# S5 mixer: the exchanged state inputs from a second product instead of transfers between partitions

## The chip, the core and the metric

The kernel runs on one core of a Trainium2 chip. The metric is the device time of one execution in microseconds (us). TensorE (PE) does the matrix products into PSUM, VectorE (DVE) and ScalarE (ACT) the elementwise work, GpSimd (POOL) a few small operations and some transfers, and SyncE (SP) issues most transfers (DMA). Each engine takes its own instructions in the order of its queue.

## The reference, cut to what matters

Two layers run over 1024 positions of 1024 channels in float32. Layer 0 mixes the positions with S5, layer 1 with a short convolution; after each mixer come a SwiGLU network and a gated embedding. Only the S5 mixer is touched. Each of 64 groups of 16 channels drives 64 complex states:

```python
bu_re = jnp.einsum('bcgk,gpk->bcgp', u_c, bb_re)
bu_im = jnp.einsum('bcgk,gpk->bcgp', u_c, bb_im)
acum_re, acum_im, hl_re, hl_im = lax.associative_scan(
    _scan_combine, (a_seq_re, a_seq_im, bu_re, bu_im), axis=1)
...
y = (jnp.einsum('bcgp,gkp->bcgk', hs_re, c_re)
     - jnp.einsum('bcgp,gkp->bcgk', hs_im, c_im))
```

## The kernel before

The positions are cut into 128 blocks of 8, so that the recurrence runs over 128 block states instead of 1024 positions. The 64 groups are worked through in 8 bands of 8 groups (`GB = 8`, `NBT = 8`, the index is `b`). In a band, the 128 partitions of a state tile hold the 64 real parts (`R0`) and the 64 imaginary parts (`R1`).

For each band these functions are called, in the order of the loop that is printed below:

- `gen_in(b)` (L831) scales and transposes the input into `U` (ACT L836, PE L842, ACT L845), forms the input matrix on DVE (two L575 into `raw`), transposes it on PE (L855, 16 instructions) and copies it out of PSUM on ACT in two halves (L857) into `wbt`.
- `states(b)` (L903) multiplies `wbt` and `U` into `pb`, two PSUM banks (L906, 8 products, each of two instructions).
- `scan(b)` (L909) turns the states into a real recurrence. A rotation by the phase tables `E` needs each part's partner: DVE multiplies `pb` with the sine into `tm` (a `tmp` tile, two L579), two transfers on SP's queue (`swapped`, L641) exchange the upper and lower 64 partitions into `tw`, DVE multiplies `pb` with the cosine into `sv` (two L575) and adds `tw` (one L575). Then eight recurrences (L925) write `gv`, and four more DVE operations rotate back, into a `tmp` tile that outputs read and into `gv`.
- `gen_out(b)` (L859) forms the output matrix `W1` (three L575 of 1024 columns) and, by L874 on PE, L876 on ACT and L880 on POOL, the direct term `kp`. `gen_swap` (L882) makes `W2` by two transfers (L886), `gen_toeplitz` (L889) spreads `kp` into `M` by eight (L893), `gen_phase` (L895) spreads the phase table into `E` by four on POOL's queue (L900). `phases` (L810) makes the table for two bands on DVE.
- `outputs(b)` (L933) sums three products for each group, with `M` (L940), `W1` (L941) and `W2` (L942), 48 PE instructions in a band, and `channels(b, zt)` (L947) transposes the result into the next operand.

`up_product(1)` (L466) is other work of the kernel that has the lowest priority and fills PE in this stage: each piece is six matmuls of 512 columns (L122 to L124 into `pstu`, a pool of one PSUM bank), an ACT copy (L478) and a transfer (L479).

The order within each queue is not written out. The framework's scheduler takes it from a simulated timeline: the instruction that is ready and has the highest priority goes first, and priority falls with the place in the program. PSUM has eight banks: three in pool `tr`, one in `tu`, and two tiles of two banks in `mb`. `gv`, `sv`, `M`, `W2`, `wbt` and `tw` have one buffer each; `U`, `W1`, `E` and `tmp` have two.

After the loop `glu` begins with casts of its weights (L87 into `uhigh`) and TensorE-bound products.

Of the kernel before, what the change touches and what calls it, by code (L numbers as in the profile page):

```python
# [9 lines left out]
F32 = mybir.dt.float32  # L10
# [4 lines left out]
ALU = mybir.AluOpType  # L15
PSUM = bass.MemoryType.PSUM
DRAM = bass.MemoryType.DRAM

P = 128
# [4 lines left out]
def trunk(  # L24
# [8 lines left out]
    V, A, G, PE = nc.vector, nc.scalar, nc.gpsimd, nc.tensor  # L33
# [15 lines left out]
    big = ctx.enter_context(tc.tile_pool(name="big", bufs=1))  # L49
    tr = ctx.enter_context(tc.tile_pool(name="tr", bufs=3, space=PSUM))  # L50
    tu = tc.alloc_tile_pool(name="tu", bufs=1, space=PSUM)
    mb = tc.alloc_tile_pool(name="mb", bufs=2, space=PSUM)
    dram = ctx.enter_context(tc.tile_pool(name="dram", bufs=1, space=DRAM))

    ident = const.tile([P, P], F32, name="ident")
# [26 lines left out]
    def psum(pool=None):  # L82
        pool = pool or mm
        return pool.tile([P, 512], F32, name="ps" + pool.name, tag="ps")
# [7 lines left out]
    def raw_tile(i=None, shape=(P, D), dt=F32, name="raw"):  # L92
        if i is None:
            slots.append(slots.pop(0))
        tag = slots[-1] if i is None else f"r{i}"
        return (uhp if tag == "r3" else rawp).tile(list(shape), dt, name=name, tag=tag)
# [451 lines left out]
    R0, R1 = slice(0, NP), slice(NP, P)  # L548
    GB = P // KG
# [11 lines left out]
    gen = tc.alloc_tile_pool(name="s5g", bufs=1, side="right")  # L561
# [12 lines left out]
    def tt(o, a, b, op):  # L574
        V.tensor_tensor(o, a, b, op)  # L575
        return o

    def stt(o, a, s, b, op0, op1):
        V.scalar_tensor_tensor(o, a, s, b, op0, op1)  # L579
        return o  # L580
# [58 lines left out]
    def swapped(dst, src):  # L639
        for a, c in ((R0, R1), (R1, R0)):  # L640
            nc.sync.dma_start(out=dst[a], in_=src[c])  # L641
# [3 lines left out]
    for hf in range(2):  # L645
        pt = psum(tr)
# [5 lines left out]
    for hf in range(2):  # L652
        pt = psum(tr)
# [148 lines left out]
    sv = run.tile([P, GB, P], F32, name="sv")  # L802
# [4 lines left out]
    def tmp_tile():  # L807
        return run.tile([P, GB * P], F32, name="tmp", tag="tmp", bufs=2)
# [20 lines left out]
    Us, Ws, W2s, Es, Bs, wbts, Ps, kps, Ms = {}, {}, {}, {}, {}, {}, {}, {}, {}  # L829

    def gen_in(b):  # L831

        gsl = slice(b * GB, (b + 1) * GB)
        xg = raw_tile(0).rearrange("p (g t k) -> p g t k", g=GB, t=T)
        for t in range(T):
            A.activation(xg[:, :, T - 1 - t, :], h[t][:, b * P:(b + 1) * P].rearrange("p (g k) -> p g k", k=KG),  # L836
                         AF.Copy, scale=rstd[:, t:t + 1])
        U = Us[b] = run.tile([P, GB, P], F32, name="U", tag="U", bufs=2)
        for hf in range(2):
            pt = psum(tr)  # L840
            for c in range(4):
                PE.transpose(pt[:, c * P:(c + 1) * P], xg[:, 4 * hf + c].rearrange("p t k -> p (t k)"), ident)  # L842
            for c in range(4):
                g = 4 * hf + c
                A.activation(U[:, g, :], pt[:, c * P:(c + 1) * P], AF.Copy, scale=gk[:, b * GB + g:b * GB + g + 1])  # L845
        shp = [P, GB, T, KG]
        Wp = [raw_tile(i).rearrange("p (g t k) -> p g t k", g=GB, t=T) for i in (1, 2)]
        for o, pw, bb in ((Wp[0], pwr, bbA), (Wp[1], pwn, bbS)):
            tt(o, pw[:, gsl, 0:T].unsqueeze(3).broadcast_to(shp), bb[:, gsl].unsqueeze(2).broadcast_to(shp), ALU.mult)
        wbt = wbts[b] = gen.tile([P, GB, P], F32, name="wbt", tag="wbt")  # L850
        for hf in range(2):
            pt = psum(tr)
            for c in range(4):
                for i in range(2):
                    PE.matmul(pt[:, c * P:(c + 1) * P], Wp[i][:, 4 * hf + c].rearrange("p s k -> p (s k)"), ident,  # L855
                              start=i == 0, stop=i == 1, is_transpose=True)
            A.copy(wbt[:, 4 * hf:4 * hf + 4].rearrange("p c n -> p (c n)"), pt)  # L857

    def gen_out(b):  # L859

        gsl = slice(b * GB, (b + 1) * GB)
        shp = [P, GB, NL, KG]
        W1 = Ws[b] = run.tile(shp, F32, name="W1", tag="W1", bufs=2)
        A.copy(W1[:, :, 0, :], cA[:, gsl])
        shp1 = [P, GB, T, KG]
        tm = tmp_tile()[:, 0:GB * P].rearrange("p (g s k) -> p g s k", g=GB, s=T)
        for o, pw, cc in ((W1[:, :, 1:NL, :], pwr, cA), (tm, pwn, cS)):
            tt(o, pw[:, gsl, 1:NL].unsqueeze(3).broadcast_to(shp1), cc[:, gsl].unsqueeze(2).broadcast_to(shp1), ALU.mult)
        tt(W1[:, :, 1:NL, :], W1[:, :, 1:NL, :], tm, ALU.subtract)
        kp = kps[b] = gen.tile([KG, GB, T, KG], F32, name="kp", tag="kp")  # L870
        for hf in range(2):
            pk = psum(tr)
            for c in range(4):
                PE.matmul(pk[0:KG, c * P:(c + 1) * P], bbA[:, b * GB + 4 * hf + c, :], W1[:, 4 * hf + c, 0:T, :],  # L874
                          start=True, stop=True)
            A.copy(kp[:, 4 * hf:4 * hf + 4].rearrange("p g s k -> p (g s k)"), pk[0:KG, :])  # L876
        dd = gen.tile([KG, GB, KG], F32, name="dd", tag="dd")
        G.tensor_tensor(dd, ident[:KG, :KG].unsqueeze(1).broadcast_to([KG, GB, KG]),
                        dk[:, gsl].unsqueeze(2).broadcast_to([KG, GB, KG]), ALU.mult)
        G.tensor_tensor(kp[:, :, 0, :], kp[:, :, 0, :], dd, ALU.add)  # L880
# [20 lines left out]
                                    in_=ptabs[b // LB][two * NP:(two + 1) * NP, :, o:o + HQ, :])  # L901

    def states(b):  # L903
        pb = mb.tile([P, GB * P], F32, name="pb", tag="pb")
        for g in range(GB):
            PE.matmul(pb[:, g * P:(g + 1) * P], wbts[b][:, g, :], Us[b][:, g, :], start=True, stop=True)  # L906
        Bs[b] = pb.rearrange("p (g j) -> p g j", g=GB)

    def scan(b):  # L909
        B = Bs[b]  # L910
        C, S_ = Es[b][:, 0], Es[b][:, 1]
        parts = ((slice(0, NJ - 1), slice(1, NJ), slice(NJ - 1, 0, -1), sgnN, sgnA),
                 (slice(NJ - 1, P - 1), slice(NJ, P), slice(0, NJ), sgnA, sgnN))
        tm = tmp_tile()[:, 0:GB * (P - 1)]
        tv = tm.rearrange("p (g j) -> p g j", g=GB)
        for j, _, m, _, sg in parts:
            stt(tv[:, :, j], B[:, :, j], sg, S_[:, :, m], ALU.mult, ALU.mult)
        tw = gen.tile([P, GB * (P - 1)], F32, name="tw", tag="tw")
        swapped(tw, tm)
        for j, w, m, _, _ in parts:  # L920
            tt(sv[:, :, w], B[:, :, j], C[:, :, m], ALU.mult)
        tt(sv[:, :, 1:P], sv[:, :, 1:P], tw.rearrange("p (g j) -> p g j", g=GB), ALU.add)
        for g in range(GB):
            dec = r8[:, b * GB + g:b * GB + g + 1].broadcast_to([P, P - 1])
            V.tensor_tensor_scan(gv[:, g, 1:P], dec, sv[:, g, 1:P], 0.0, ALU.mult, ALU.add)  # L925
        pv = Ps[b] = tmp_tile().rearrange("p (g j) -> p g j", g=GB)
        G.memset(pv[:, :, 0:1], 0.0)
        for _, w, m, sg, _ in parts:
            tt(pv[:, :, w], gv[:, :, w], C[:, :, m], ALU.mult)
        for _, w, m, sg, _ in parts:  # L930
            stt(gv[:, :, w], gv[:, :, w], sg, S_[:, :, m], ALU.mult, ALU.mult)
# [15 lines left out]
    def channels(b, zt):  # L947
        for hf in range(2):
# [3 lines left out]
            split_pe(v[:, :, b, 0, hf, :], v[:, :, b, 1, hf, :], pt, by_kt)  # L952

    gen_in(0)
    phases(0)
    states(0)
    gen_phase(0)
    gen_out(0)
    gen_swap(0)
    gen_toeplitz(0, M)  # L960
    gen_in(1)
    for b in range(NBT):
        scan(b)
        nx = b + 1
        if nx < NBT - 1:
            if b % LB == 0 and b // LB + 1 < NBT // LB:
                phases(b // LB + 1)
            gen_out(nx)
            zt = outputs(b)
            gen_phase(nx)  # L970
            states(nx)
            gen_swap(nx)
            gen_toeplitz(nx, M)
            if b + 2 < NBT:
                gen_in(b + 2)
            channels(b, zt)
        elif nx < NBT:
            states(nx)
            gen_phase(nx)
            gen_out(nx)  # L980
            M = run.tile([P, GB, P], F32, name="M", tag="E", bufs=2)
            G.memset(M, 0.0)
            gen_toeplitz(nx, M)
            zt = outputs(b)
            channels(b, zt)
            gen_swap(nx)
        else:
            zt = outputs(b)
# [111 lines left out]
```

## Time and profile before

| | us |
|---|---|
| median of 3 runs | 2356.54 |
| lowest and highest | 2355.79, 2357.86 |
| the profiled execution | 2359.43 |
| its span, first to last instruction | 2357.5 |

| engine | busy us | share of the span |
|---|---|---|
| TensorE matmul (PE) | 2247.0 | 95% |
| TensorE weight load (PEld) | 1835.7 | 78% |
| VectorE (DVE) | 1331.9 | 56% |
| ScalarE (ACT) | 765.5 | 32% |
| GpSimd (POOL) | 163.1 | 7% |

Busy times are those of the engines' own instructions. A matmul of 128 columns is shown with 0.27 us or more although the next one starts about 0.11 us after it, so a busy TensorE is not one at its peak. Idle time of an engine that sets no pace costs nothing. The bands of S5 lie between about 55 and 225 us of the span. The profiled execution took 1.93 us more than its span.

### The profile page before, as it was taken

How to read it: one execution, taken by the hardware profiler on the slowest of the kernel's cores; microseconds unless marked ns; L12 is line 12 of the kernel's file. 1: busy time of each engine (PE TensorE's matmuls, PEld its weight loads, DVE VectorE, ACT ScalarE, POOL GpSimd, SP SyncE). 2: the span in 40 equal slices, each digit the busy share in tenths (PEclk: the TensorE clock that was granted, in tenths of full speed). 3: DMA queues.
4: the chain of work that ended last, by engine and by line, in shares of the span. 5: the costliest groups of instructions: out<-in, count | busy, mean ns of one | idle time of the engine just before them, and what ended most of it. 6: DMA issues, size and time to landing. Idle time of an engine off the chain costs nothing.

```text
span 2357.5 us, 27090 instructions
## 1 busy us (share of the span) xinstructions
PE 2247.0 (95%) x10253; PEld 1835.7 (78%) x10253; DVE 1331.9 (56%) x2246; ACT 765.5 (32%) x1449; POOL 163.1 (7%) x268
## 2 busy tenths in 40 slices
PE   6888999899999999999979999989999999999998
PEld 4776887788888878878858888768888888788787
DVE  7785326866666642125488776487666666121454
ACT  6554223433333320013343332153333333000232
POOL 2110001000000000000000000010000001000000
PEclk8999999999999999999989999999999999999999
DMA  7555202333333364333232225434333335543333
GB/s 246 141 135 148 69 1 89 105 112 112 111 114 110 107 241 149 118 127 114 70 129 81 90 92 179 159 125 125 108 108 107 111 113 172 212 139 107 108 109 110
DMA packets 212978, 288.87 MB, mean 123 GB/s; under 512 B 21360, under 2 KB 152432, under 8 KB 212848
## 3 DMA queue, kind: packets, MB, share of 16 engines
q1 hardware_dynamic: 191520, 212.63, 29.0%
q0 software_dynamic: 20928, 74.47, 10.2%
q8 instruction: 80, 1.31, 0.2%
q14 instruction: 50, 0.41, 0.1%
q10 hardware_dynamic: 400, 0.04, 0.0%
HBM read 190.93 MB, written 79.69 MB: 115 GB/s over the span
## 4 chain that ended last, share of the span: by engine, by line
PE 85%; DMA 6%; DVE 5%; ACT 1%; SPq 1%; issue 1%; POOL 0%; DVEq 0%; POOLq 0%; ACTq 0%
PE psmm L122 27%; PE psmm L124 27%; PE psmm L123 27%; DMA ch<-hid 2%; PE pstr L181 1%; DMA raw<-in_ffn_w_out_dram 1%; DMA tw<-tmp 1%; DVE W L575 1%; DVE gv L925 1%; DMA h<-hd 1%; DVE tmp L575 1%; DVE ulow L88 1%; DVE uhigh L88 1%; PE pstr L874 0%; DVE raw L575 0%
## 5 line engine op out<-in xcount | busy, mean ns | idle before, releaser
L122 PE MATMUL psmm<-ulow,ws 128*128 128x512 f32 x896 | 351.1, 393 | 1.6 <-ACT s L301 1.6
L123 PE MATMUL psmm<-ulow,ws 128*128 128x512 f32 x896 | 350.6, 391 | 0.0
L124 PE MATMUL psmm<-ulow,ws 128*128 128x512 f32 x896 | 350.4, 391 | 0.0
L124 PE MATMUL psmm<-uhigh,ws 128*128 128x512 f32 x672 | 265.3, 395 | 0.0
L122 PE MATMUL psmm<-uhigh,ws 128*128 128x512 f32 x672 | 265.1, 394 | 0.0
L123 PE MATMUL psmm<-uhigh,ws 128*128 128x512 f32 x672 | 264.9, 394 | 0.0
L360 DVE TENSOR_TENSOR h<-psmm,h 128x512 f32<-128x512 f32 x128 | 88.0, 690 | 276.6 <-PE psmm L124 276.6
L88 DVE TENSOR_TENSOR ws<-raw,ws 128x512 fp32r<-128x512 f32 x224 | 153.6, 688 | 117.8 <-ACT ws L87 117.4
L87 ACT CAST ws<-raw 128x512 fp32r<-128x512 f32 x224 | 137.5, 619 | 213.0 <-PE psmm L124 211.2
L122 PEld LDWEIGHTS psmm<-ulow,ws 128*128 128x128 f32 x896 | 169.4, 189 | 39.5 <-ACT s L301 2.9
L123 PEld LDWEIGHTS psmm<-ulow,ws 128*128 128x128 f32 x896 | 169.4, 189 | 36.2
L124 PEld LDWEIGHTS psmm<-ulow,ws 128*128 128x128 f32 x896 | 169.2, 189 | 36.2
L87 ACT CAST ws<-st 128x512 fp32r<-128x512 f32 x168 | 104.0, 620 | 204.4 <-PE psmm L124 189.5
L123 PEld LDWEIGHTS psmm<-uhigh,ws 128*128 128x128 f32 x672 | 126.1, 188 | 30.3
L124 PEld LDWEIGHTS psmm<-uhigh,ws 128*128 128x128 f32 x672 | 126.1, 188 | 30.3
L122 PEld LDWEIGHTS psmm<-uhigh,ws 128*128 128x128 f32 x672 | 126.1, 188 | 29.1
L323 POOL DMA_DIRECT2D hid<-hs x104 | 78.2, 755 | 903.4 <-DVE hs L88 895.4
L122 PE MATMUL psmm<-ulow,ch 128*128 128x512 f32 x320 | 128.4, 401 | 10.8 <-DMA ch<-hid 10.8
L139 ACT ACTIVATE junk<-h 128x512 bf16<-128x512 f32 (+1 forms) x113 | 64.0, 567 | 204.0 <-DVE h L360 104.0
L87 ACT CAST uhigh<-raw 128x1024 fp32r<-128x1024 f32 x36 | 37.2, 1049 | 278.9 <-PE psmm L124 136.7
L123 PE MATMUL psmm<-ulow,ch 128*128 128x512 f32 x320 | 127.6, 399 | 0.0
L124 PE MATMUL psmm<-ulow,ch 128*128 128x512 f32 x320 | 127.5, 398 | 0.0
(240 smaller groups left out, 4238.5 us busy)
## 6 DMA issues: line engine op xcount, KB each, us to landing
hid<-hs POOLq DMA_DIRECT2D x104, 512.0 KB, 4.3
ch<-hid SPq DMA_DIRECT2D x96, 512.0 KB, 3.7
raw<-in_ffn_w_in_dram SPq DMA_DIRECT2D x88, 512.0 KB, 4.4
raw<-in_ffn_w_out_dram SPq DMA_DIRECT2D x44, 512.0 KB, 3.6
hd<-h POOLq DMA_DIRECT2D x24, 512.0 KB, 3.0
h<-hd SPq DMA_DIRECT2D x24, 512.0 KB, 8.7
raw<-in_conv_w_in_dram SPq DMA_DIRECT2D x24, 512.0 KB, 4.0
up<-ev SPq DMA_DIRECT2D x32, 256.0 KB, 3.2
```

Source lines behind the costliest of these rows:

```text
L87: A.copy(hi, src)
L88: V.tensor_tensor(lo, src, hi.bitcast(F32), ALU.subtract)
L122: PE.matmul(ps, ahi, bhi, start=start, stop=False, skip_group_check=more)
L123: PE.matmul(ps, ahi, blo, start=False, stop=False, skip_group_check=more)
L124: PE.matmul(ps, alo, bhi, start=False, stop=stop, skip_group_check=more)
L139: A.activation(junk[:, cs], h[t][:, cs], AF.Square, scale=1.0 / math.sqrt(D), accum_out=ms)
L181: PE.transpose(pt[:, c * P:(c + 1) * P], xn[:, kt * P:(kt + 1) * P], ident)
L323: nc.gpsimd.dma_start(out=hid[ht // 4][half * HT:(half + 1) * HT, :, ht % 4].rearrange("t p l j -> p t l j"), in_=hs.bitcast(F32))
L360: V.tensor_tensor(h[t][:, cs], ps[nb], h[t][:, cs], ALU.add)
L575: V.tensor_tensor(o, a, b, op)
L925: V.tensor_tensor_scan(gv[:, g, 1:P], dec, sv[:, g, 1:P], 0.0, ALU.mult, ALU.add)
```

## The change

The input matrix is kept twice: `wbt` as before, and `wbs` with the real and imaginary columns exchanged, which four more ACT copies of 128 x 256 in a band read from the same PSUM tiles. `wbs` takes the buffer of `tw`. `states` makes two products with the same `U`, first `qb` with `wbs`, then `pb` with `wbt`. `qb` and `pb` have one buffer each instead of two of `pb`, so that `mb` keeps four banks. `scan` multiplies `qb` with the sine, with the signs of the other set of `parts`, and adds the result without a transfer.

```diff
-    mb = tc.alloc_tile_pool(name="mb", bufs=2, space=PSUM)
+    mb = tc.alloc_tile_pool(name="mb", bufs=1, space=PSUM)
...
-        wbt = wbts[b] = gen.tile([P, GB, P], F32, name="wbt", tag="wbt")
+        wbt, wbs = wbts[b] = [gen.tile([P, GB, P], F32, name=n, tag=g) for n, g in (("wbt", "wbt"), ("wbs", "tw"))]
...
             A.copy(wbt[:, 4 * hf:4 * hf + 4].rearrange("p c n -> p (c n)"), pt)
+            pv = pt.rearrange("p (c n) -> p c n", c=4)
+            for o, i in ((R0, R1), (R1, R0)):
+                A.copy(wbs[:, 4 * hf:4 * hf + 4, o], pv[:, :, i])
...
     def states(b):
-        pb = mb.tile([P, GB * P], F32, name="pb", tag="pb")
-        for g in range(GB):
-            PE.matmul(pb[:, g * P:(g + 1) * P], wbts[b][:, g, :], Us[b][:, g, :], start=True, stop=True)
-        Bs[b] = pb.rearrange("p (g j) -> p g j", g=GB)
+
+        Bs[b] = []
+        for i, n in ((1, "qb"), (0, "pb")):
+            pb = mb.tile([P, GB * P], F32, name=n, tag=n)
+            for g in range(GB):
+                PE.matmul(pb[:, g * P:(g + 1) * P], wbts[b][i][:, g, :], Us[b][:, g, :], start=True, stop=True)
+            Bs[b].insert(0, pb.rearrange("p (g j) -> p g j", g=GB))
 
     def scan(b):
-        B = Bs[b]
+        B, Bw = Bs[b]
...
-        for j, _, m, _, sg in parts:
-            stt(tv[:, :, j], B[:, :, j], sg, S_[:, :, m], ALU.mult, ALU.mult)
-        tw = gen.tile([P, GB * (P - 1)], F32, name="tw", tag="tw")
-        swapped(tw, tm)
+        for j, _, m, sg, _ in parts:
+            stt(tv[:, :, j], Bw[:, :, j], sg, S_[:, :, m], ALU.mult, ALU.mult)
         for j, w, m, _, _ in parts:
             tt(sv[:, :, w], B[:, :, j], C[:, :, m], ALU.mult)
-        tt(sv[:, :, 1:P], sv[:, :, 1:P], tw.rearrange("p (g j) -> p g j", g=GB), ALU.add)
+        tt(sv[:, :, 1:P], sv[:, :, 1:P], tv, ALU.add)
```

## Rows read from the trace of the kernel before

**Rows 1.** The page: busy time by engine, and the chain that ended last.
```profile
PE 2247.0 (95%) x10253; PEld 1835.7 (78%) x10253; DVE 1331.9 (56%) x2246; ACT 765.5 (32%) x1449; POOL 163.1 (7%) x268
...
PE 85%; DMA 6%; DVE 5%; ACT 1%; SPq 1%; issue 1%; POOL 0%; DVEq 0%; POOLq 0%; ACTq 0%
```

**Rows 2.** Waits of DVE, 55 to 212.8 us: total us, times, longest us.
```profile
DVE sv L575 <- DMA tw<-tmp: 27.1, 8, 5.5
DVE tmp L579 <- DMA E<-ptab: 3.0, 2, 2.1
DVE ptab L813 <- DMA E<-ptab: 2.5, 1, 2.5
DVE raw L575 <- PE pstr L855: 0.3, 1, 0.3
```

**Rows 3.** Timeline of DVE, band 4: start, us, instruction, idle before and releaser.
```profile
138.74 0.74 DVE L579 SCALAR_TENSOR_TENSOR tmp<-pb,sgnA,E 128x504 f32<-128x504 f32 x1
139.51 0.75 DVE L579 SCALAR_TENSOR_TENSOR tmp<-pb,sgnN,E 128x512 f32<-128x512 f32 x1
140.18 1.27 DVE L575 TENSOR_TENSOR sv<-pb,E 128x504 f32<-128x504 f32 x2
146.83 1.22 DVE L575 TENSOR_TENSOR sv<-sv,tw 128x1016 f32<-128x1016 f32 x1 [5.38 <-DMA tw<-tmp]
```

**Rows 4.** Windows: length, busy us (instructions) by engine, granted clock, DMA share, GB/s.
```profile
55.50:212.80 157.30, 132.94 (x949) 113.69 (x947) 124.07 (x246) 82.53 (x207) 23.83 (x49) 0.99 0.60 143
...
126.20:146.80 20.60, 17.17 (x127) 14.96 (x126) 15.18 (x24) 10.83 (x29) 5.70 (x11) 1.00 0.65 160
146.80:167.50 20.70, 18.26 (x136) 15.96 (x135) 19.38 (x46) 11.85 (x33) 1.09 (x3) 1.00 0.43 100
```

**Rows 5.** Timeline of PE: one product of `states`, and what follows it.
```profile
49.90 1.95 PE L906 MATMUL pb<-U,wbt 128*128 128x128 f32 x16
51.60 0.47 PE L122 MATMUL pstu<-ulow 128*128 128x512 f32 x1
```

**Rows 6.** Waits of PE, 55.5 to 212.9 us.
```profile
PE pstr L874 <- DVE W L575: 10.2, 6, 2.4
PE pstr L940 <- DMA W<-W: 5.3, 1, 5.3
PE pstu L122 <- ACT ev L478: 5.1, 5, 1.1
PE pb L906 <- ACT wbt L857: 1.7, 1, 1.7
```

**Rows 7.** Timeline of PE: L874 of band 1 and of band 2, first half.
```profile
72.30 3.50 PE L874 MATMUL pstr<-W,bbA 128*16 128x128 f32 x16 [2.09 <-DVE W L575]
...
94.92 1.03 PE L874 MATMUL pstr<-W,bbA 128*16 128x128 f32 x8
```

**Rows 8.** Groups of ACT, 45 to 225 us, and 225 to 330 us.
```profile
L857 ACT COPY wbt<-pstr 128x512 f32<-128x512 f32 x16 | 9.0, 642 | 0.0
...
L501 ACT ACTIVATE sgg<-psmm 128x256 f32<-128x256 f32 x18 | 6.9, 382 | 44.7 <-PE psmm L124 44.7
```

**Rows 9.** Timeline of SP's queue, band 4 (start, us from first to last issue).
```profile
140.29 1.16 SPq L641 DMA_DIRECT2D tw<-tmp  x2
...
144.33 0.66 SPq L893 DMA_DIRECT2D M<-kp  x1
...
146.44 5.52 SPq L893 DMA_DIRECT2D M<-kp  x7
```

**Rows 10.** Transfers, 120 to 150 us: KB each, median us to landing.
```profile
M<-kp SPq DMA_DIRECT2D x2, 40.0 KB, 3.0
```

**Rows 11.** Timeline of PE: first product of `outputs(7)`, and of glu.
```profile
212.78 0.77 PE L940 MATMUL pstr<-M,U 128*128 128x128 f32 x2 [5.28 <-DMA W<-W]
...
225.16 1.43 PE L122 MATMUL psmm<-uhigh,ulow 128*128 128x512 f32 x5 [0.61 <-ACT uhigh L87]
```

## The prediction

> **What bounds the kernel now.** I read the page first [rows 1]: over the whole span TensorE is busy 95% and holds 85% of the chain that ended last, so a change in S5 can only move the stretch in which TensorE is not the one that is late, and everything behind the stretch follows it unshortened. Then the waits of VectorE from the first scan to the last `outputs` [rows 2]. Of its idle time there nearly all is one wait: 27.1 us, 8 times, for the exchange `tw`. The rest is 5.5 us for `E` and 0.3 us for TensorE. So VectorE never waits for TensorE here, and it sets the pace of the bands. A band shows how [rows 3]: the two sine products end at 140.26 us, the two cosine products cover 1.27 us, and the add starts at 146.83 us, after 5.38 us of nothing.
>
> Last the windows [rows 4]. The stretch from 55.5 to 212.8 us is 157.3 us long. VectorE is busy 124.07 us of it, TensorE 132.94 us, ScalarE 82.53 us. TensorE is thus the engine with the least room, 157.3 - 132.94 = 24.4 us, although it isn't the pacer: in two neighbouring bands it is busy 17.17 of 20.6 and 18.26 of 20.7 us.
>
> **Part 1, the transfers go.** Eight pairs of issues leave SP's queue (1.16 us a pair [rows 9]) and the wait of 27.1 us leaves VectorE [rows 2]. VectorE's own work does not change: the two sine products read `qb` where they read `pb`, of the same shapes, and the add reads `tm` where it read `tw`. With the wait gone its work and its other waits are 157.3 - 27.1 = 130.2 us, so VectorE alone would allow 27.1 us. The question is who is late next.
>
> **Part 2, the second product on TensorE.** One product takes 51.60 - 49.90 = 1.70 us of its queue [rows 5]. The one of band 0 lies ahead of the stretch; its scan waits for `E` (2.1 us, the longest of [rows 2]), which covers 1.70 us. If that cover were gone it would cost those 1.70 us. Seven lie inside: 7 x 1.70 = 11.9 us. TensorE's room falls to 24.4 - 11.9 = 12.5 us, and this is less than the 27.1 us that VectorE gives. TensorE becomes the bound of S5.
>
> How much of the 12.5 us comes out depends on which stops of TensorE [rows 6] stay. The six stops of L874 for `W` (10.2 us) should go: `W` stands in VectorE's queue near the eight L925, behind the add that waited for `tw`, and VectorE now runs ahead. The stop ahead of the last `outputs` (5.3 us for `W2`) stays in the main, because `W2` has one buffer and is loaded after the `outputs` before; I take off the 1.16 us that a pair of the exchange spends on the same queue [rows 9], which leaves 4.1 us. The other 24.4 - 10.2 - 5.3 = 8.9 us are short stops for ScalarE and the gaps between matmuls. The second product is something to put into them, and of these I keep a fifth, 1.8 us; that is a choice, between all gone (0) and all kept (8.9). Against this, the L874 of band 1 took 3.50 us for 16 matmuls after a pause of 2.09 us, where 8 of them take 1.03 us in band 2 [rows 7]; with no pause there 3.50 - 2 x 1.03 = 1.4 us come back.
>
> Sum: 12.5 + 1.4 - 4.1 - 1.8 = 8.0 us. With all short stops kept it is 0.9 us, with none 9.8 us.
>
> **Part 3, the copies.** Four ACT copies of 128 x 256 a band. No row of S5 has that form from PSUM to SBUF; half of the 128 x 512 copy is 0.32 us and an activation of 128 x 256 takes 0.38 us [rows 8]. I take 0.38, being the same shape: 28 x 0.38 = 10.7 us in the stretch, against 157.3 - 82.53 = 74.8 us in which ScalarE is idle [rows 4]. As time of ScalarE they cost nothing. But they stand between the transposes L855 and `states`, and they hold a bank of `tr`, of which there are three, for 0.64 + 2 x 0.38 = 1.40 us instead of 0.64 us. The bound from below is nothing, since TensorE can do `channels` or a piece of `up_product` meanwhile; the bound from above is 0.76 us for each of 14 halves, 10.6 us. I take nothing, as L906 waited for `wbt` once in the stretch, 1.7 us [rows 6], and keep 10.6 us for the range.
>
> **Part 4, buffers.** `qb` and `pb` with one buffer each make `states(b+1)` wait for the four PSUM reads of `scan(b)`. In band 4 these last from 138.74 to 141.45 us [rows 3]. No row of before shows such a wait, since there was a second buffer. From below it costs nothing, when the product comes later in the band anyway; from above the 2.7 us of the reads in a band, 18.9 us for seven, in which L906 would stand at the head of TensorE's queue with L874 and `outputs` behind it. I take nothing: the reads are the first thing that VectorE does in a scan, and with the add no longer waiting they come early in the band. `wbs` in the place of `tw` adds the wait that `wbt` has already, and no price.
>
> **A rule that speaks about the bound.** The row says that TensorE is busy 132.94 us of 157.3 and its weight loads 113.69 us [rows 4]. The Trainium skill, page "Perfetto Trace Analysis", section "Identifying the Most-Contended Engine", says that busy matmul time is a poor measure of how near TensorE is to its limit, since matmuls are pipelined, and that the share of weight loads is the better one. By that measure TensorE is at 113.69 / 157.3 = 72% and not at 85%, the seven products find room, and VectorE keeps the pace; this is the second rival below.
>
> **Rivals.**
>
> *One: TensorE is the bound and most stops go* (forecast): 8.0 us less. For it: the 24.4 us [rows 4] against the 11.9 us, and that the 10.2 us of stops hang on VectorE. Own range 0.9 to 9.8 us. Chance 0.50, of which 0.08 for less than 4.7 us.
>
> *Two: VectorE keeps the pace.* Back-to-back matmuls start 1.70 / 16 = 0.106 us apart but are shown with 1.95 us for 16 [rows 5], so each run's end counts as busy though TensorE could have started something else; and pieces of `up_product` can move behind the stretch. Then 27.1 - 4.1 = 23.0 us at most would come out, and half way between this and the 9.8 us of rival one are 16.4 us: 2340.1 us. Chance 0.15.
>
> *Three: the wait moves to `M` and `W2`.* `M` has one buffer; its first transfer follows the last read of `outputs(b)` and its seventh of the others is issued at 146.44 + 5.52 = 151.96 us in band 4 and needs some 3.0 us to land [rows 9, 10]. That is 10.6 us after 144.33. With `outputs` itself, 48 instructions at the 1.70 / 16 us of [rows 5] or 5.1 us, this loop takes about 16 us of a 20.7 us band, so it binds only in bands shortened by over 5 us; but the order is fixed from a simulated timeline, and if this has `M` land early, TensorE stops at L940 with all behind it. At 1 us a band for seven bands the 8.0 us fall to 1.0: 2355.5 us. Chance 0.17.
>
> *Four: the exchange's wait is replaced by a wait for the states themselves*, so that the scan starts later by what it saves: the change does not do what it says. The copies and the second product make 4 x 0.38 + 1.70 = 3.2 us on the way to the scan, and the wait was 27.1 / 8 = 3.4 us a band. Time as before, 2356.5 us. Chance 0.05.
>
> *Five, slower: TensorE's stops are not the exchange's.* Place: TensorE's queue in each band, between L855 and L874. If the order of VectorE's queue keeps `W` behind the eight L925 and the stops of L874, `ev` and `wbt` remain, then 7 x 1.70 = 11.9 us are added to an engine that has no room: 2368.4 us. It decides the sign as soon as more than 12.5 of the 24.4 us of idle time stay; half way, 18.4 us kept, it is 2362.5 us. Against it: VectorE waited only for transfers [rows 2]. Chance 0.13.
>
> **How the numbers follow.** The profiled execution took 2359.43 us, 1.93 us more than its span and 2.89 us more than the median of the three runs. Less 8.0 us it would be 2351.4 us; against the median, 2356.54 - 8.0 = 2348.5 us, which is the forecast. The glu stage begins at 225.16 us right behind the last band [rows 11] and is shifted whole. A measurement of this kernel can tell about 0.2% from no change, here 4.7 us. Faster by more than that: 0.42 of rival one, all of two, 0.03 of three: 0.60. Within it: 0.08 + 0.14 + 0.05 = 0.27, from which I move 0.01 to slower for copies that hold `tr` on top. Slower: 0.14. The range reaches from 2338.0 us, a little beyond the middle of rival two (0.06 left out below), to 2359.0 us, past no change by the noise of one execution (0.12 left out above, most of rival five).
>
> **What would show it.** `tw` and L641 are gone from S5, and L575 `sv` has no wait. L906 counts 256 instead of 128. TensorE's busy time from the first scan to the last `outputs` rises by about 12 us while the stretch falls from 157.3 to about 149 us; L874's stops for `W` are under 3 us in total. Rival two shows as a stretch below 142 us with VectorE without idle time. The last `outputs` still stops some 4 us for `W2` [rows 11]. Rival three shows as stops of L940 for `M` or `W` in several bands, five as L874's stops unchanged. The prediction fails most easily by the order that the scheduler gives the pieces of `up_product`, which nothing in the rows fixes.

## The result and the profile after

| | before | after |
|---|---|---|
| median of 15 runs, us | 2356.56 | 2361.60 |
| lowest and highest, us | 2347.55, 2358.14 | 2356.32, 2363.75 |
| ratio to before, 95% interval | | 1.0022 [1.0014, 1.0030] |
| the profiled execution, us | 2359.43 | 2361.6 |
| its span, us | 2357.5 | 2359.7 |

The change makes the kernel 5.0 us slower; 2348.5 us was forecast, with a range up to 2359.0 us. In the kernel after, `states` is L912, the copies into `wbs` are L860, L874 has become L877, and the three products of `outputs` are L944 to L946.

The page of the kernel after, busy time by engine and the chain that ended last, as [rows 1]:
```profile
PE 2260.4 (96%) x10381; PEld 1852.2 (78%) x10381; DVE 1335.7 (57%) x2246; ACT 774.7 (33%) x1481; POOL 161.9 (7%) x268
...
PE 86%; DMA 4%; DVE 2%; ACT 1%; issue 0%; POOL 0%; SPq 0%; POOLq 0%; DVEq 0%; ACTq 0%
```
TensorE has 128 instructions more and 13.4 us more busy time, and the shares of transfers and of VectorE in the chain went down, from 6 to 4% and from 5 to 2%. The windows view of the bands, from the first scan to the first product of `outputs(7)`, as the first line of [rows 4] (length, busy us and instructions of PE, PEld, DVE, ACT and POOL, granted clock, DMA share, GB/s):
```profile
55.50:213.70 158.20, 145.53 (x1073) 127.12 (x1071) 127.00 (x246) 90.96 (x235) 24.21 (x50) 0.99 0.50 120
```
The stretch did not shrink from 157.3 us: it is 158.2 us long, and TensorE's idle time in it fell from 24.4 to 158.20 - 145.53 = 12.7 us. The waits of TensorE in the same stretch (total us, times, longest), as [rows 6]:
```profile
PE pstu L122 <- ACT ev L478: 5.4, 5, 1.1
PE pstr L944 <- DMA W<-W: 4.0, 1, 4.0
PE pstr L877 <- DVE W L575: 1.3, 1, 1.3
PE pb L912 <- ACT wbt L857: 1.0, 1, 1.0
```
And those of VectorE, as [rows 2]:
```profile
DVE tmp L579 <- PE qb L912: 13.6, 5, 4.2
DVE gv L929 <- PE pstr L946: 8.0, 22, 1.6
DVE tmp L579 <- DMA E<-ptab: 3.0, 1, 3.0
DVE sv L575 <- PE pb L912: 2.3, 1, 2.3
```
The 27.1 us of waiting for `tw` are gone, and VectorE waits for TensorE instead: 13.6 + 2.3 us for the states and 8.0 us for the last reads of `outputs`, which hold `gv`. Before, it waited for TensorE 0.3 us. TensorE's stops for `W` fell from 10.2 to 1.3 us. So the pacer changed as forecast, and the time did not.

The groups of TensorE and ScalarE, 45 to 225 us of the kernel after (busy us, mean ns, idle before):
```profile
L912 PE MATMUL qb<-U,wbs 128*128 128x128 f32 x128 | 18.0, 278 | 0.0
L912 PE MATMUL pb<-U,wbt 128*128 128x128 f32 x128 | 17.9, 277 | 1.0 <-ACT wbt L857 1.0
L860 ACT COPY wbs<-pstr 128x256 f32<-128x256 f32 x32 | 11.6, 457 | 0.0
L857 ACT COPY wbt<-pstr 128x512 f32<-128x512 f32 x16 | 10.5, 655 | 0.0
```
And one product of `states`, its two halves interleaved in eights, in the timeline of TensorE (start, us, instruction):
```profile
50.62 1.06 PE L912 MATMUL pb<-U,wbt 128*128 128x128 f32 x8
51.51 1.06 PE L912 MATMUL qb<-U,wbs 128*128 128x128 f32 x8
52.41 1.06 PE L912 MATMUL pb<-U,wbt 128*128 128x128 f32 x8
```
Eight instructions take 0.89 us of the queue, a product of sixteen 1.78 us, against the 1.70 us of [rows 5].

### The profile page after: what moved, and what is told of

Same layout as the page of the kernel before. It is cut to its first block, busy times and chain, and to the rows that moved or that the text cites. A ratio compares the mean times of both kernels' runs of the same rounds, so it can differ in the third digit from the quotient of the medians.

```text
span 2359.7 us, 27352 instructions
## 1 busy us (share of the span) xinstructions
PE 2260.4 (96%) x10381; PEld 1852.2 (78%) x10381; DVE 1335.7 (57%) x2246; ACT 774.7 (33%) x1481; POOL 161.9 (7%) x268
## 3 DMA queue, kind: packets, MB, share of 16 engines
q0 software_dynamic: 20928, 74.47, 10.2%
## 4 chain that ended last, share of the span: by engine, by line
PE 86%; DMA 4%; DVE 2%; ACT 1%; issue 0%; POOL 0%; SPq 0%; POOLq 0%; DVEq 0%; ACTq 0%
PE psmm L122 28%; PE psmm L124 27%; PE psmm L123 27%; DMA ch<-hid 2%; PE pstr L181 1%; DMA raw<-in_ffn_w_out_dram 1%; DMA raw<-in_ffn_w_in_dram 1%; DVE uhigh L88 1%; DMA h<-hd 0%; PE pstr L944 0%; ACT uhigh L87 0%; PE pstr L945 0%; PE pstr L946 0%; DVE ulow L88 0%; DMA W<-W 0%
## 5 line engine op out<-in xcount | busy, mean ns | idle before, releaser
L122 PE MATMUL psmm<-ulow,ws 128*128 128x512 f32 x896 | 351.9, 394 | 2.2 <-ACT s L301 1.3
L122 PE MATMUL psmm<-uhigh,ws 128*128 128x512 f32 x672 | 265.1, 395 | 0.0
L122 PEld LDWEIGHTS psmm<-ulow,ws 128*128 128x128 f32 x896 | 169.6, 189 | 40.4 <-ACT s L301 2.4
L122 PEld LDWEIGHTS psmm<-uhigh,ws 128*128 128x128 f32 x672 | 126.2, 188 | 29.0
L122 PE MATMUL psmm<-ulow,ch 128*128 128x512 f32 x320 | 129.1, 403 | 10.4 <-DMA ch<-hid 10.2
```

The costliest lines, as they stand in the source:

```text
L122: PE.matmul(ps, ahi, bhi, start=start, stop=False, skip_group_check=more)
```

## The experiments

**Theory A:** once the exchange's wait is gone TensorE is the bound of S5; the transfers were worth some 10 us, and the second product costs its whole time, since the idle time of TensorE is not room. **Its rivals**, lettered in the expectations: the second product is hidden where TensorE is idle, and what was won is lost by the copies, by waits inside the bands, or behind S5. What each run tells apart stands in its expectation.

### free: what the transfers were worth

The kernel before without the transfers, and nothing in their place.

```diff
-        tw = gen.tile([P, GB * (P - 1)], F32, name="tw", tag="tw")
-        swapped(tw, tm)
...
-        tt(sv[:, :, 1:P], sv[:, :, 1:P], tw.rearrange("p (g j) -> p g j", g=GB), ALU.add)
+        tt(sv[:, :, 1:P], sv[:, :, 1:P], tv, ALU.add)
```

> The kernel before without the two transfers, and with nothing in their place: the add reads the products unexchanged, so the exchange of real and imaginary parts is left out of what is computed. No second product, no copies. Theory A (in S5 TensorE is the bound as soon as the transfers go, and the second product takes back what they give): without the product TensorE keeps its 24.4 us of room, of which the last stop for W2 (4 us) and the stops for ev (5 to 6 us) stay, so 10 to 14 us less than before, 2343 to 2347 us. Rival B (the wait for the exchange hid nothing and the loss of the change is the order that the later stages get): within 3 us of before, 2354 to 2360 us.

Measured: 2346.47 us, ratio to before 0.9950 [0.9934, 0.9965], 10.7 us less. The profiled execution is the fastest of its four (2341.22 us), so its trace shows more gain than the median. Its bands in the windows view, 55.5 us to the first product of the last `outputs`:
```profile
55.50:199.10 143.60, 130.92 (x950) 113.19 (x948) 126.22 (x246) 82.81 (x207) 26.12 (x50) 0.99 0.53 131
```
Its waits of VectorE there:
```profile
DVE tmp L579 <- PE pb L906: 5.7, 3, 2.4
DVE gv L923 <- PE pstr L940: 5.2, 12, 2.1
```
And glu's first product in its timeline, 14.3 us earlier than in [rows 11]:
```profile
210.82 1.42 PE L122 MATMUL psmm<-uhigh,ulow 128*128 128x512 f32 x5 [0.61 <-ACT uhigh L87]
```
Even without the second product VectorE waits for TensorE, 10.9 us, and TensorE is idle only 143.60 - 130.92 = 12.7 us. That is as much as in the kernel after, which has 15.1 us more time: 2361.6 - 2346.5. What the transfers were worth is spent on the second product, and more.

### double: the second product while the exchange still sets the pace

The kernel before, with the transfers, and the product of `states` made twice into the same tile.

```diff
-        for g in range(GB):
+        for g in [*range(GB), *range(GB)]:
             PE.matmul(pb[:, g * P:(g + 1) * P], wbts[b][:, g, :], Us[b][:, g, :], start=True, stop=True)
```

> The kernel before, transfers kept, with every product of the states made twice into the same banks: only TensorE's 8 x 1.70 = 13.6 us are added. Theory A: VectorE still paces with its wait for the exchange, TensorE's room takes in part of it; 4 to 10 us more than before, 2360 to 2366 us, if the products stand on the way from the copies to the scan (1.70 us a band), and no more than 13.6. Rival B: TensorE has room enough and the product is hidden, within 3 us of before.

Measured: 2369.64 us, 1.0054 [1.0037, 1.0071], 12.5 us more, which is beyond the 4 to 10 us expected. The windows view of its bands (the profiled execution took 2367.13 us):
```profile
55.50:224.60 169.10, 147.40 (x1068) 128.44 (x1065) 125.10 (x246) 82.87 (x206) 23.68 (x48) 0.99 0.57 136
```
Its waits of VectorE in them:
```profile
DVE sv L575 <- DMA tw<-tmp: 19.0, 7, 5.1
DVE tmp L579 <- PE pb L906: 6.0, 2, 4.6
DVE gv L925 <- PE pstr L942: 4.8, 7, 3.3
```
This is the run that the forecast's reasoning doesn't survive. Eight products more, 8 x 1.70 = 13.6 us, went to an engine with over 20 us of idle time in a stretch that another engine paces, and 12.5 us of them came out at the end. VectorE's wait for `tw` fell to 19.0 us (27.1 and 23.6 us in two traces of before), and 10.8 us of waits for TensorE came. The longest is 4.62 us for `pb`, in a band in which four pieces of `up_product` stand between 183.4 us and the states' product at 196.3 us. That the scheduler piles them up there is seen and not controlled.

### nocopies: what the copies and `wbs` cost

The kernel after, both products made from `wbt`, no copies L860.

```diff
-        wbt, wbs = wbts[b] = [gen.tile([P, GB, P], F32, name=n, tag=g) for n, g in (("wbt", "wbt"), ("wbs", "tw"))]
+        wbt = gen.tile([P, GB, P], F32, name="wbt", tag="wbt")
+        wbts[b] = [wbt, wbt]
...
-            pv = pt.rearrange("p (c n) -> p c n", c=4)
-            for o, i in ((R0, R1), (R1, R0)):
-                A.copy(wbs[:, 4 * hf:4 * hf + 4, o], pv[:, :, i])
```

> The changed kernel without the four ACT copies a band: the second product reads the plain matrix, so the exchange is left out of what is computed. Theory A (TensorE's product is the price): within 2 us of the changed kernel, 2359 to 2363 us. Rival C (the copies hold the three banks of tr and stand in front of the states): 28 copies x 0.3 us or more come back, 2351 to 2356 us.

Measured: 2362.97 us, 1.0025 [1.0015, 1.0036] to before, so the time of the kernel after. The copies took 11.6 us of ScalarE and no time of the kernel that shows; as the cause of the loss they fall. A price of one or two us isn't excluded, because this kernel has another order (its stops for `ev` are 8.0 us in the bands, those of the kernel after 5.4). Beside free, the second product, with one buffer each for `qb` and `pb`, costs 2362.97 - 2346.47 = 16.5 us here.

### shift: the exchange by neither transfer nor product

The kernel before; each sine product is cut into two of 64 partitions, one half read and the other half written.

```diff
         for j, _, m, _, sg in parts:
-            stt(tv[:, :, j], B[:, :, j], sg, S_[:, :, m], ALU.mult, ALU.mult)
-        tw = gen.tile([P, GB * (P - 1)], F32, name="tw", tag="tw")
-        swapped(tw, tm)
+            for o, i in ((R0, R1), (R1, R0)):
+                stt(tv[o, :, j], B[i, :, j], sg[i], S_[i, :, m], ALU.mult, ALU.mult)
...
-        tt(sv[:, :, 1:P], sv[:, :, 1:P], tw.rearrange("p (g j) -> p g j", g=GB), ALU.add)
+        tt(sv[:, :, 1:P], sv[:, :, 1:P], tv, ALU.add)
```

> The exchange made by VectorE itself: each of the two sine products a band is split into two of 64 partitions, which read one half of the partitions and write the other; no transfer, no second product, no copies. Price 2 more instructions of 0.67 us a band on VectorE, 10.7 us, against its wait of 27.1 us; TensorE's work as before. Theory A: TensorE keeps its room of 24.4 us and VectorE gains 16.4 us, so 7 to 12 us less than before, 2345 to 2350 us. Rival B: no gain, 2354 to 2360 us.

Measured: 2348.82 us, 0.9960 [0.9945, 0.9975], 8.3 us under before: it beats both kernels. The windows view of its bands (the profiled execution is the fastest of four, 2345.43 us):
```profile
55.50:202.30 146.80, 132.89 (x955) 114.05 (x954) 136.63 (x262) 82.65 (x207) 24.64 (x52) 1.00 0.54 130
```
One of its two new groups of VectorE by tile (ns: shortest, median, longest; first and last start):
```profile
L579 DVE SCALAR_TENSOR_TENSOR tmp<-pb,sgnN,E x16: 743/750/757, 58.5 to 189.6; 64x512 f32<-64x512 f32 x16
```
Its waits of TensorE in the bands, the longest in total:
```profile
PE pstu L122 <- ACT ev L478: 6.9, 7, 1.1
```
And of VectorE:
```profile
DVE gv L924 <- PE pstr L941: 1.2, 5, 0.2
DVE tmp L579 <- PE pb L906: 1.0, 2, 0.8
```
The exchange now costs VectorE 136.63 - 124.07 = 12.6 us and TensorE nothing. VectorE waits 2.2 us for TensorE. The exchange is paid on the engine that had been waiting, and 8.3 of the 10.7 us that free shows are kept.

### thin_before and thin_after: is it TensorE?

Both kernels with every piece of `up_product(1)` cut to its first matmul of three, some 14.7 us of TensorE less.

```diff
+                        if l == 1:
+                            PE.matmul(ps, up_room(l, kt, 0)[:, sl], up_room(l, PKT + kt, 0)[:, cs],
+                                      start=kt == 0, stop=kt == PKT - 1)
+                            continue
```

> The kernel before with up_product(1) cut from three matmuls to the first of the three (two corrections left out of what is computed, 16 pieces x 4 x 0.23 us = 14.7 us of TensorE): the low-priority filler of S5 shrinks by as much as the second product adds. Theory A (VectorE's wait for the exchange paces the stage before the change, TensorE has room): little gain, 0 to 5 us, 2352 to 2357 us. Rival B (TensorE paced S5 before already): 10 us or more, under 2347 us.

> The changed kernel with the same cut of up_product(1). Theory A: with 14.7 us of TensorE's work gone the change shows what the transfers were worth; 8 to 12 us less than the changed kernel, 2349 to 2354 us, and 3 to 8 us less than the kernel before with the same cut. Rival B (the loss sits in the later stages, or in copies and buffers): no faster than the cut kernel before, by more than 2 us slower.

Measured: thin_after 2353.21 us, 8.4 us under the kernel after, as A has it. thin_before 2361.55 us, 1.0022 [1.0013, 1.0031]: slower than before by 5.3 us with 14.7 us less to do, which no theory expected. The timeline of SP's queue in its band from 136.4 to 165.4 us, 29 us long:
```profile
143.68 7.03 SPq L897 DMA_DIRECT2D M<-kp  x7
150.80 1.18 SPq L645 DMA_DIRECT2D tw<-tmp  x2
```
And that of VectorE in the same band:
```profile
141.81 1.23 DVE L579 TENSOR_TENSOR W<-pwr,cc 128x1024 f32<-128x1024 f32 x1 [4.75 <-issue]
...
155.53 1.22 DVE L579 TENSOR_TENSOR sv<-sv,tw 128x1016 f32<-128x1016 f32 x1 [5.08 <-DMA tw<-tmp]
```
The second sine product ended at 143.72 + 0.75 = 144.47 us, but the exchange was issued at 150.80 us behind seven issues of `M`, and VectorE stood still twice, 4.75 us for nothing that the profile names and 5.08 us for the exchange. TensorE lost time in another way. The windows view of the bands:
```profile
55.50:215.70 160.20, 126.41 (x886) 108.05 (x885) 123.80 (x246) 82.17 (x207) 25.23 (x49) 0.91 0.59 141
```
It has 61 instructions less than before3 (947, below), at 0.23 us each some 14 us, but its busy time is only 132.52 - 126.41 = 6.1 us less, because the granted clock was 0.91 and not 0.99. The timeline of TensorE in the band above:
```profile
148.45 3.33 PE L910 MATMUL pb<-U,wbt 128*128 128x128 f32 x16
151.44 1.04 PE L475 MATMUL pstu<-ulow 128*128 128x512 f32 x2
```
The product of `states` took 151.44 - 148.45 = 2.99 us of the queue instead of 1.70 us [rows 5]. TensorE had stood still for 2.03 us shortly before, and the granted clock from 148 to 166 us was 0.62, a mean over its two levels of 1.2 and 2.4 GHz. So over half of what was cut came back as slower work. The thinner pieces changed the scheduler's order as well, so thin_before doesn't tell the theories apart. It does show what the transfers on a shared queue can cost. The pair thin_before and thin_after, 8.3 us apart in favour of the change, is spoilt by that band and by the clock as well.

### The same two kernels again

No edit; three more traces of each, for how much S5 and what follows it move by themselves.

> The kernel before once more, for a second trace, as with the changed one: glu at 225.2 us within 0.5 us, later stages as far apart from the first trace as the theories say.

> The changed kernel once more, for a second trace: the glu stage should start within 0.5 us of 224.7 us if the stretch repeats, and the rest of the kernel shows how much its stages move from execution to execution. Theory A: the later stages move by 1 us or more each between two executions of the same order. Rival B: the later stages repeat to 0.3 us, so that their differences from the kernel before are due to the order.

> The kernel before, a third trace. Theory A (before the change S5 waits eight times for transfers whose time varies, so its end varies; after it TensorE paces and the end repeats): glu starts anywhere between 217 and 226 us, the rest of the kernel takes 2130 to 2138 us. Rival B (the time that the change adds lies in the stages behind S5): glu at 221 to 225 us, the rest 2130 us or less.

> The changed kernel, a third trace. Theory A: glu at 223 to 225 us, the rest of the kernel 2130 to 2138 us as before the change. Rival B: the rest 2134 us or more in each trace, over that of the kernel before.

> The kernel before, a fourth trace, with the expectations of the third.

> The changed kernel, a fourth trace, with the expectations of the third.

Glu's first product in the timeline of TensorE (start, us), in before2:
```profile
221.37 1.42 PE L122 MATMUL psmm<-uhigh,ulow 128*128 128x512 f32 x5 [0.60 <-ACT uhigh L87]
```
In before3:
```profile
220.95 1.42 PE L122 MATMUL psmm<-uhigh,ulow 128*128 128x512 f32 x5 [0.61 <-ACT uhigh L87]
```
And in after3, the latest of all:
```profile
226.97 1.43 PE L122 MATMUL psmm<-uhigh,ulow 128*128 128x512 f32 x5 [0.60 <-ACT uhigh L87]
```
All eight traces, from these rows and from the waits of TensorE in S5, in us:

| | before | before2 | before3 | before4 | after | after2 | after3 | after4 |
|---|---|---|---|---|---|---|---|---|
| glu starts | 225.16 | 221.37 | 220.95 | 221.42 | 224.71 | 223.16 | 226.97 | 224.12 |
| TensorE's stops for `W` (L874, L877) | 10.2 | 7.0 | 6.0 | 7.1 | 1.3 | 1.6 | 1.1 | 0.8 |
| its stop ahead of the last `outputs` | 5.3 | 4.9 | 5.1 | 5.0 | 4.0 | 3.7 | 5.3 | 3.6 |
| its stops for `ev` (L122) | 5.1 | 5.1 | 5.3 | 5.1 | 5.4 | 5.5 | 5.5 | 5.4 |
| span from glu's start on | 2132.3 | 2138.0 | 2132.4 | 2131.3 | 2135.0 | 2134.7 | 2132.5 | 2130.8 |

What follows S5 takes 2133.5 us on the mean before and 2133.2 after: nothing is lost behind S5, and that rival falls, though a single trace can differ by 7 us there. The expected repeats failed: before2 has glu 3.8 us from 225.2, after2 1.5 us from 224.7, and after3 lies outside 223 to 225 us, so the end of S5 doesn't repeat better with TensorE as the pacer. S5 itself ends at 221.2 us in three traces of before, and at 224.7 us on the mean of the four after: 3.5 us later. The trace on which the prediction rests is the odd one: its S5 ended 3.9 us later than the other three, and its stops for `W` are 3.5 us longer than their mean of 6.7 us.

before3 is a usual one. The windows view of its bands:
```profile
55.50:208.70 153.20, 132.52 (x947) 114.13 (x945) 123.39 (x246) 82.51 (x207) 23.79 (x48) 0.99 0.61 146
```
Its waits of TensorE in them:
```profile
PE pstr L874 <- DVE W L575: 6.0, 4, 2.4
PE pstu L122 <- ACT ev L478: 5.3, 6, 1.1
PE pstr L940 <- DMA W<-W: 5.1, 1, 5.1
PE pb L906 <- ACT wbt L857: 2.2, 1, 2.2
```
Against it the stretch of the kernel after is 158.2 - 153.2 = 5.0 us longer: TensorE's work grew by 145.53 - 132.52 = 13.0 us and its idle time fell from 20.7 to 12.7 us, by 8.0.

### tr2_after and tu_after: what holds the short stops

The stops for `ev` are the same before and after. `pstu` has one PSUM bank, so that a piece of `up_product` right behind another waits for ScalarE's copy. All eight banks are in use, so one is taken from `tr`, and in tu_after it is given to `tu`. The diff is that of tu_after; tr2_after leaves `tu` at one.

```diff
-    tr = ctx.enter_context(tc.tile_pool(name="tr", bufs=3, space=PSUM))
-    tu = tc.alloc_tile_pool(name="tu", bufs=1, space=PSUM)
+    tr = ctx.enter_context(tc.tile_pool(name="tr", bufs=2, space=PSUM))
+    tu = tc.alloc_tile_pool(name="tu", bufs=2, space=PSUM)
```

> The kernel after with pool tr cut from three PSUM banks to two and nothing put in the free bank: the companion of tu_after, which gives the bank to tu. It shows what the third bank of tr is worth by itself. Theory A (short stops of TensorE are held by the one bank of pstu): the stops of L122 for ev stay at about 5.4 us in the stretch; with one bank less for transposes and outputs some new stops come, 0 to 5 us: 2361 to 2366 us. Theory B (stops only change their name): the same, 2361 to 2366 us. Prices of tr are not what the two differ in; they differ in tu_after against this one.

> The kernel after with pool tr cut to two banks and tu given two, so that a piece of up_product need not wait until ScalarE has copied the one before it. Theory A (the short stops that I took for filled are held by the one bank of pstu; the work that could stand in them is the next piece itself): the stops of L122 for ev fall from 5.4 us to under 1.5 us in the stretch, TensorE's idle time there falls by about 4 us against tr2_after, and the time is 3 to 5 us under tr2_after. Theory B (TensorE has nothing else ready at those places, and the order that the scheduler gives puts the idle time elsewhere): the stops for ev go, but others of the same total come (wbt, zt, W2 or M), idle time within 1.5 us of tr2_after, time within 2 us of it. If only B holds, my step on the short stops failed by more than one bank.

Measured: tr2_after 2383.41 us, 1.0107 [1.0089, 1.0125]; tu_after 2374.64 us, 1.0075 [1.0060, 1.0090]. Waits of TensorE from 45 us to glu's start in tr2_after:
```profile
PE pb L912 <- ACT wbt L857: 7.2, 6, 1.7
PE pstu L122 <- ACT ev L478: 5.3, 5, 1.5
```
And in tu_after:
```profile
PE pb L912 <- ACT wbt L857: 7.8, 5, 1.7
...
PE pstu L122 <- ACT ev L478: 1.0, 2, 0.7
```
The second bank takes the stops for `ev` from 5.3 to 1.0 us, and the kernel is 8.8 us faster than tr2_after. So the one bank holds these stops, as the first theory of this pair has it. The windows view from 45 us to glu, tr2_after first:
```profile
45.00:244.22 199.22, 174.19 (x1214) 150.88 (x1212) 139.96 (x258) 105.84 (x274) 37.10 (x60) 0.96 0.44 107
45.00:232.50 187.50, 167.12 (x1199) 146.57 (x1197) 136.53 (x256) 105.29 (x272) 38.13 (x60) 0.97 0.45 110
```
TensorE's idle time fell from 25.0 to 20.4 us, 4.6 less, as this theory has it. The 3 to 5 us that it expected of the whole time are passed by some 4 us, and these come with another order: TensorE did 14 instructions more before 45 us, 15 less after it, and its busy time is 7.1 us less there. The third bank of `tr`, with the order that goes with it, is worth far more, 2383.41 - 2361.60 = 21.8 us where up to 5 were expected, so the bank can't be had there.

## Why the prediction was wrong

Its sum set beside the trace of after, for TensorE from 55.5 us to the first product of `outputs(7)`:

| us | before [rows 4, 6] | forecast | after |
|---|---|---|---|
| busy | 132.9 | 132.9 + 11.9 - 1.4 = 143.4 | 145.5 |
| stops for `W` | 10.2 | 0 | 1.3 |
| stop for `W2` | 5.3 | 4.1 | 4.0 |
| the other idle time | 8.9 | 1.8 | 7.4 |
| length | 157.3 | 149.3 | 158.2 |

**What was right.** TensorE becomes the bound: VectorE's waits say so. The stops for `W` go with the exchange. The stop ahead of the last `outputs` stays, at 4.0 us for 4.1. The copies cost nothing that shows, though one takes 457 ns and not 380, and in none of the four traces of after does L912 stop for VectorE's reads of `qb` and `pb` (Part 4). Rival three didn't come: of L944 the waits show one stop. Rival four came in part: VectorE waits 13.6 + 2.3 us for the states. But the copies aren't the reason, since the first of these waits is 14.5 us in nocopies; TensorE is late. Rival two would have needed pieces of `up_product` behind the stretch; there are 52 matmuls of L122 in S5 before and after.

**The step that failed first** is "of these I keep a fifth, 1.8 us" (Part 2). 7.4 of the 8.9 us stayed, 5.6 us of the miss of 8.9. The row was at hand: 5.1 us of the 8.9 are the five stops of L122 for `ev` [rows 6]. These are stops at the head of an in-order queue for a PSUM bank, and another product further back in the queue can't be put into them; tu_after shows that a bank does. I had called them a thing to fill without asking what each waits for. My own lower end, all of them kept, was 0.9 us of gain.

**The rest of the table.** 1.3 us are a stop for `W` that stayed, in band 1. 2.1 us are TensorE's work: the second product of band 0, ahead of the stretch, pushed five matmuls of 512 columns of `up_product` (145 in the stretch for 140) and six of L874 past 55.5 us, 5 x 0.23 + 6 x 0.12 = 1.9 us by their places in the timeline; besides, a product took 1.78 us and not 1.70. Most of the pushed work is not a loss, since the part from `outputs(7)` to glu is 1.3 us shorter: 224.71 - 213.65 = 11.1 us against 225.16 - 212.78 = 12.4 us [rows 11].

**The second step that failed** is the base. I took one trace's idle time as the kernel's, and in "How the numbers follow" moved the whole gain over to the median by subtracting 2.89 us from both sides. That trace was late in S5 itself: 3.5 us of its 10.2 us of stops for `W` are not there in the others. It took 2359.43 us, more than the slowest of the 15 runs (2358.14 us). Its stretch is 157.3 - 153.2 = 4.1 us longer than before3's, and these 4.1 us come on top of the miss of 8.9.

The 1.4 us to be given back were about right, for another band. The slow L874 of band 1 (16 matmuls in 3.50 us [rows 7], 1.92 us in before3, with a granted clock of 0.90, a mean over both its levels of 1.2 and 2.4 GHz, and 1.00 between 66 and 83 us) is not there in the others, but these have a slow stretch in another place: from 130 to 137 us the granted clock was 0.76 in all three. In the four traces of after it was 1.00 from 45 to 205 us. So TensorE's busy time from 45 us to glu grew by 164.0 - 152.2 = 11.8 us on the mean of four traces, where eight products of 1.70 us are 13.6 us.

Made on before3 with the other idle time kept, the sum is 20.7 - 11.9 us of room, and 1.4 us given back, less 5.1 - 1.2 us for `W2`, less 20.7 - 6.0 - 5.1 = 9.6 us of other stops: -3.3 us, slower. Measured in that stretch: 5.0 us slower, of which some 1.2 us came back behind it, since glu starts 224.71 - 220.95 = 3.8 us later. This sum was made after the result and is no test; it shows that the two steps are enough to turn the sign.

**The rule on the bound.** By weight loads TensorE stood at 72% before [rows 4], which the Trainium skill, page "Perfetto Trace Analysis", section "Identifying the Most-Contended Engine", names, beside the share of the peak arithmetic rate (MFU), as a better measure than busy matmul time. Here it read as room that wasn't there: double went from 72% to 128.44 / 169.10 = 76% and lost 12.5 us, and the kernel after, with VectorE waiting for TensorE, stands at 127.12 / 158.20 = 80%. The 92% of busy matmuls and the stops between them account for the whole stretch.

**Rival five** had the sign and not the reason. Its bound was met by a hair, as 12.7 us of idle time are left and more than 12.5 were to decide the sign. But it let the stops of L874 stay; these went, and the product and the stops for `ev` took their place.

**What is open.** The medians differ by 5.0 us, with an interval of 3.3 to 7.1 us, the ends of S5 by 3.5 us (2.5 with the odd trace); with ends that vary by 4 us from trace to trace, the rest isn't settled. Why the first trace of before was late isn't known. One buffer each for `qb` and `pb` was not varied by itself: the 16.5 us between nocopies and free are 2.3 us more than eight products of 1.78 us, and these may be the buffers or the order. Why the pieces of `up_product` pile up in one band in double, or SP's issues in thin_before, is the scheduler's order and wasn't varied by itself.

## What to carry to other kernels

Before you call an engine's idle time room, list its waits: a stop at the head of its own queue for a buffer or a bank does not take in other work, and one that hangs on the thing you remove can be won only once. When a transfer is replaced by arithmetic, put it on the engine that waits, not on the one that is next in line: against 2346.5 us with no exchange at all, the exchange cost 15 us as a product on TensorE with its copies, and 2.4 us where VectorE's two sine products were each split into two half-width operations. And take the base from several traces: one trace here was 3.9 us late in the very stretch that was to be shortened.

## What the runs showed of the hardware

- A VectorE operation on 64 partitions takes as long as one on 128: 750 ns for 64 x 512 in shift, 0.75 us for 128 x 512 [rows 3]. It can read one half of the partitions from PSUM and write the other half of an SBUF tile at no extra time, which makes the exchange cost a second operation: VectorE's busy time grew by 12.6 us for 16 operations of 0.75 us.
- ScalarE's copy of 128 x 256 from PSUM into runs of 64 columns took 457 ns, and the copy of 128 x 512 beside it 655 ns: half the columns, 70% of the time.
- TensorE's granted clock fell where its queue had stops. In thin_before it stood still for 2.03 us, and from 148 to 166 us, with stops of 3.88 and 1.95 us inside, the granted clock was 0.62, between its levels of 1.2 and 2.4 GHz; a product of `states` took 2.99 us there for 1.70 us. Taking 14 us of work out of TensorE took 6.1 us off its busy time.
- With the transfers in the kernel the end of S5 lay between 220.95 and 225.16 us in four traces of one program. Without them it did not become steadier: 223.16 to 226.97 us after.
